# A trunk of four encoder layers on one core: settling an mLSTM head between the next one's reciprocal and additions, and the first and last chunks cut finer

## The chip, the cores and the metric

The kernel runs on 1 core of one Trainium2 chip. A core has TensorE (PE in the profile; PEld is its weight load), VectorE (DVE), ScalarE (ACT), GpSimd (POOL) and SyncE (SP), each of which works in order through its own queue, and 16 DMA engines. The metric is device time in microseconds (us) of one execution. Before the change it was 927.92 us, the median of 3 runs (927.56 to 928.36).

## What is computed

The input x has 256 tokens of 1024 features in float32. Two layers of three sublayers each follow; every sublayer is added to a scaled x and normalised. In layer 0 the mixer is a bidirectional mLSTM with 4 heads, in layer 1 a windowed attention:

```python
for l in range(DEPTH):                                       # DEPTH = 2
    x = layer_norm(ALPHA * x + 0.5 * swiglu(x, ffn_w_in[l, 0], ffn_w_out[l, 0]), ...)
    y = mlstm_mixer(...) if l % 2 == 0 else window_attention(...)
    x = layer_norm(ALPHA * x + y, ...)
    x = layer_norm(ALPHA * x + 0.5 * swiglu(x, ffn_w_in[l, 1], ffn_w_out[l, 1]), ...)
```

`swiglu` is `(silu(x @ Wg) * (x @ Wu)) @ w_out` with 2816 hidden features. In the mLSTM each head has 256 value features and two directions. With `num` and `den` of both directions, a head's output is

```python
h = num_f / max(|den_f|, e_f) + num_b / max(|den_b|, e_b)
h = (h - mean(h)) * rsqrt(var(h) + LN_EPS)                    # per token and head
out = sigmoid(o) * (h * norm_g);  y = out @ w_out
```

## The kernel before

**Number format and tiles.** Each float32 operand is cut into a high and a low part (`_hi`, `_lo`, type fp32r), and a product is three matmuls: high by high, high by low, low by high (`mm3`, L476). Tokens lie in two tiles of 128 (`xt[0]`, `xt[1]`); `xT_hi` and `xT_lo` hold the features on the partitions, made by transposes on TensorE against `ident` (`to_xT`, L505), after which ScalarE copies the high part and VectorE subtracts for the low one (`split_evac`, L495). PSUM tiles come from two rings of four banks, `pw` (`wbank`) and `py` (`ybank`).

**Weights.** `Weights` (L147) holds the list of all weight pieces, 128 x 1024 numbers (512 KB) each, in the order of use. SyncE loads them into a ring (`w_raw`, 4 buffers); ScalarE copies each into `w_hi` (`high`, L214) and VectorE makes `w_lo` (`low`, L238), after which the buffer is free and the next load is issued. For the very first piece, `high` and `low` work in two halves of 512 columns. Inside the feed-forward sublayers a planner (`Paced`, L52) counts costs of the instructions as they are written and decides where the next `w_hi` and `w_lo` go in the engines' order; elsewhere the order is written by hand, with `W.done(0, n)` or `spare()` as places where up to n pieces are split. All queues are worked off in order.

**Start.** ScalarE's queue issues the four loads of x (a half of 512 features of a token tile each), SyncE's queue the first weights. TensorE does 14 transposes of `ident` by itself (`warm(14)`), 4 of the first half of `xt[0]`, 8 more of `ident`, and then the first products of the first weight piece (`first_mm`, L629). The high part of that half of x is copied by VectorE, not by ScalarE, in this place alone.

**mLSTM heads (L1078 on).** The loop over the 4 heads h writes: a piece of the output gate's projection on TensorE, `scores(h)` (with `combine(h - 2)` inside), `mix(h - 1)`, `divide(h - 1)`, `settle(h - 2)`. In `mix` TensorE makes the four numerators (2 token tiles, 2 directions) and ScalarE the absolute denominators. In `divide` VectorE takes the maximum and the reciprocal, ScalarE scales the first direction into `hx`, and VectorE adds the second direction scaled (2 instructions of 128x256). `combine` makes mean and variance of a head on VectorE (`hst`, `hmv`, `hrs`), and POOL raises to the power -1/2. `settle` subtracts the mean and multiplies by that power, in place, on VectorE (2 instructions of 128x256). After the loop come `divide(3)`, `combine(3)`, `settle(2)`, the product with the output gate's sigmoid (`gate_out`, tiles `h<-h,sg`), `settle(3)` and, from L1112, the transposes of `hx[0]` and the output projection.

**End of a sublayer (`tail`, L559).** Each token tile's output is 128 x 1024 in two PSUM banks, `y[t][0]` and `y[t][1]` (512 columns each), summed over the last chunks in `todo` (6 of them at the very end, three matmuls each per half). For tile 1 the order is: the second half's first 3 chunks, the first half's 6, the second half's last 3. `Norm.half` (L533) adds a half to the scaled x and takes its statistics (`bn_stats`); `Norm.finish` (L538) combines them (`mv`), lets POOL make the power (`rs`), and applies the gain `ln_g` and the offset `ln_b` on VectorE. In the last sublayer both are done in two pieces of 512 columns, and SyncE stores each piece (`out_dram`).

Of the kernel before, what the change touches and what calls it, by code (L numbers as in the profile page):

```python
# [9 lines left out]
F32 = mybir.dt.float32  # L10
FR = mybir.dt.float32r
AF = mybir.ActivationFunctionType
OP = mybir.AluOpType
# [133 lines left out]
class Weights:  # L147
# [66 lines left out]
    def high(self):  # L214

        nc, i = self.nc, self.made
        p = self.plan[i]
        while self.half and (p["word"] not in self.raw or any(h[0] == p["needs"] for h in self.half)):
            self.low()
        while any(s_[0] == p["needs"] or p["word"] not in self.raw for s_ in self.sums):  # L220
            self.sum()
        if p["word"] not in self.raw:
            return False
        scale, raw = p["scale"], self.raw[p["word"]]
        hi = self.pool.tile([128, D], FR, name="w_hi", tag="w_hi", bufs=RING)
        if i == 0:
            for j in range(2):
                s_ = slice(j * 512, j * 512 + 512)
                nc.scalar.copy(hi[:, s_], raw[:, s_])
        elif scale is None:  # L230
            nc.scalar.copy(hi, raw)
        else:
            nc.scalar.activation(hi, raw, AF.Copy, scale=scale())
        self.half.append((i, hi))
        self.made += 1
        return True

    def low(self):  # L238

        nc = self.nc  # L240
        i, hi = self.half.pop(0)
        p = self.plan[i]
        k, scale, raw = p["k"], p["scale"], self.raw[p["word"]]
        lo = self.pool.tile([128, D], FR, name="w_lo", tag="w_lo", bufs=RING)
        if i == 0:
# [75 lines left out]
def trunk_kernel(ctx: ExitStack, tc: tile.TileContext, x, ffn_w_in, ffn_w_out, ln_g, ln_b, ml_w_in, ml_gate_b,  # L321
# [67 lines left out]
    for j, (kind, l, i, _) in enumerate(stages):  # L389
        if kind == "ffn":  # L390
            wi, wo = ffn_w_in[l, i], ffn_w_out[l, i]
            nth = iter(range(2 * UNITS))

            def down(n):
                for _ in range(n):
                    rows(wo, next(nth))

            for c0 in (0, F):
                for a in range(4):
                    wide(wi, a * 256, c0)  # L400
            for g in range(GROUPS):
                c0 = 512 + 768 * g
                for a in range(4):
                    beside(wi, a * 256, c0, F + c0)
                down(2)
                seven(wi, c0 + 256, F + c0 + 256, lambda i_: down(1) if g < GROUPS - 1 or i_ < 2 else None)
            down(6)
        elif kind == "mlstm":
            for c0 in (1024, 1536):
                for a in range(4):  # L410
                    wide(ml_w_in[0], a * 256, c0)
            for c0 in range(0, 1024, 256):
                for a in range(2):
                    narrow(ml_w_in[0], a * 512, c0)
            for c0 in (2048, 2560):
                for a in range(4):
                    wide(ml_w_in[0], a * 256, c0)
            for c in range(8):
                rows(ml_w_out[0], c, (lambda c=c: gcol[:, c:c + 1]))
        else:  # L420
            for c0 in (1024, 0):
                for a in range(4):
                    wide(at_w_in[0], a * 256, c0)
            for c0 in (512, 768):
# [103 lines left out]
    class Norm:  # L528
        def __init__(self, t, ca, eps, gb, last=False):
            self.t, self.ca, self.eps, self.gb, self.last = t, ca, eps, gb, last  # L530
            self.stats = state.tile([128, 2, 6], F32, name="stats", tag="stats", bufs=2)

        def half(self, h, y):  # L533
            z = xt[self.t][:, h * 512:(h + 1) * 512]
            nc.vector.scalar_tensor_tensor(z, z, self.ca, y, op0=OP.mult, op1=OP.add)
            nc.vector.bn_stats(self.stats[:, h], z)

        def finish(self, spare):  # L538
            mv = state.tile([128, 2], F32, name="mv", tag="mv", bufs=2)
            nc.vector.bn_aggr(mv, self.stats)  # L540
            rs = state.tile([128, 2], F32, name="rs", tag="rs", bufs=2)
            nc.vector.tensor_scalar(rs[:, 0:1], mv[:, 1:2], self.eps, None, op0=OP.add)
            nc.gpsimd.tensor_tensor(rs[:, 1:2], rs[:, 0:1], mhalf[:, 0:1], op=OP.pow)
            z = xt[self.t]
            cuts = [slice(0, 512), slice(512, D)] if self.last or self.t and LC[bound[0]] else [A]
            for s_ in cuts:
                nc.vector.scalar_tensor_tensor(z[:, s_], z[:, s_], mv[:, 0:1], self.gb[0][:, s_],
                                               op0=OP.subtract, op1=OP.mult)
            if len(cuts) == 1:
                W.done(0, spare)  # L550
            for s_ in cuts:
                nc.vector.scalar_tensor_tensor(z[:, s_], z[:, s_], rs[:, 1:2], self.gb[1][:, s_],
                                               op0=OP.mult, op1=OP.add)
                if self.last:
                    nc.sync.dma_start(out[0, tok(self.t), s_], z[:, s_])
            if len(cuts) > 1:
                W.done(0, spare)

    def tail(y, h, todo, first, norm, last, turn_at, between=None):  # L559

        def one(t, o, n):
            c, (i, w) = todo[t][n]
            mm3(y[t][o], h(c, t), pair(w, A, 0, slice(o * 512, o * 512 + 512)), first and n == 0, n == len(todo[t]) - 1)

        for o in range(2):
            for n in range(len(todo[0])):
# [9 lines left out]
        for j, (o, n) in enumerate(order):  # L576
            if j == full + turn_at:
                emit_x(0, last)
            one(1, o, n)
            if j >= half and (n < half) == (o == 0):  # L580
                W.done(todo[1][n][1][0] + 1, next(more))
            if n == full - 1:
                norm[1].half(o, y[1][o])
        norm[1].finish(1)
        W.done(most=TD[bound[0]])
        return lambda: emit_x(1, last)
# [5 lines left out]
    def ffn(l, i, n, pending, last):  # L592
        with ExitStack() as ph:
# [10 lines left out]
            start = pending is None  # L604
            if start:
                warm(14)
                to_xT(0, xt[0], ybank, (0,), nc.vector.tensor_copy)
                W.split(1)
                warm(8)
            hs, pieces = [], []  # L610

            def tr(hB, t, h):
# [15 lines left out]

            def first_mm(ps, a):  # L629

                def mm(t, i, j):
                    for k in (2 * a, 2 * a + 1):
                        nc.tensor.matmul(ps[t], xT[i][:, k, tok(t)], pieces[a][j][:, k % 2], start=i == j == k == 0,
                                         stop=False)

                if a == 1:
                    for t in range(2):
                        to_xT(t, xt[t], ybank, (1,))
                pieces.extend(W.take(1))
                mm(0, 0, 0)  # L640
                if a == 0:
                    to_xT(1, xt[1], ybank, (0,))
                    W.split(2)
                mm(0, 1, 0)
# [222 lines left out]
    def mlstm(l, n, pending, last):  # L867
        with ExitStack() as ph:
# [157 lines left out]
                        ys.append(y)  # L1026
                part[h] = den, ys

            def divide(h):
                den, ys = part.pop(h)  # L1030
                nc.vector.tensor_max(den, den, ecol[:, :, h:64:32])
                nc.vector.reciprocal(den, den)
                for t in range(2):
                    nc.scalar.activation(hx[t][:, h], ys[2 * t][:, 0:256], AF.Copy, scale=den[:, t, 0:1])
                for t in range(2):
                    hh = hx[t][:, h]
                    nc.vector.scalar_tensor_tensor(hh, ys[2 * t + 1][:, 0:256], den[:, t, 1:2], hh,
# [40 lines left out]
            for h in range(4):  # L1078
# [332 lines left out]
```

## Time and profile before

| | |
|---|---|
| median of 3 runs | 927.92 us (927.56 to 928.36) |
| the profiled execution | 928.32 us |
| its span, first to last instruction | 926.6 us |
| TensorE busy | 916.5 us (99%), 4506 matmuls |
| VectorE, ScalarE, POOL busy | 785.4, 544.4, 98.1 us |
| mean granted TensorE clock | 0.997 |
| from HBM | 185.68 MB |

A row of the timeline gives start and duration in us, engine, line, operation, tile written and tiles read, shapes, a count of merged instructions (x2), and in brackets the idle time of the engine before it with what ended it. Nearly all rows have line L138, that of a helper which records every operation, so groups are told apart by their tiles. Matmuls are pipelined: one row's duration overlaps the next, and the distance between starts is what one costs. A row of the stretches gives from and to, length, busy time and count of PE, PEld, DVE, ACT and POOL, granted clock, DMA share and GB/s. A row of one tile's view gives the shortest, median and longest duration in ns. The chain that ended last is followed back from the last instruction, at each step to what released it.

### The profile page before, as it was taken

The page shows a single profiled execution, that of the slowest core. Times are in us where ns is not written, and L with a number is a line of the kernel's source. Part 1 is how long each engine was busy: PE and PEld are TensorE (multiplying, and loading weights), DVE is VectorE, ACT ScalarE, POOL GpSimd, SP SyncE. Part 2 cuts the span into 40 slices and gives each one's busy share as a digit, 9 for nine tenths or more (in the row PEclk, how much of TensorE's full clock was granted, in tenths as well). Part 3 has the DMA queues.
Part 4 walks back from the last instruction along what each step waited for, and adds up shares of the span by engine and source line. Part 5 has one row for each costly group of instructions (what it writes and reads, how often), then busy time and mean ns, then how long its engine had stood idle before and what let it go on. Part 6 is the DMA issues. An engine that isn't in the chain of part 4 may idle for free.

```text
span 926.6 us, 12512 instructions
## 1 busy us (share of the span) xinstructions
PE 916.5 (99%) x4506; PEld 767.3 (83%) x4506; DVE 785.4 (85%) x948; ACT 544.4 (59%) x766; POOL 98.1 (11%) x144
## 2 busy tenths in 40 slices
PE   9999999999999999999999999999999999999996
PEld 7888888889988888888888888888888888888885
DVE  5899997886699799988887899988868878998875
ACT  5656756347664548565636566565569555757460
POOL 0010103011111010101010101010435300110100
PEclk9999999999999999999999999999999999999998
DMA  8979774646535949685558597737434385969421
GB/s 280 356 180 334 216 246 74 229 133 199 188 108 188 344 112 345 166 304 137 160 176 323 144 330 210 269 69 227 156 122 133 101 273 195 274 194 346 122 86 45
DMA packets 98461, 187.54 MB, mean 202 GB/s; under 512 B 6720, under 2 KB 37456, under 8 KB 98400
## 3 DMA queue, kind: packets, MB, share of 16 engines
q1 hardware_dynamic: 91072, 173.04, 54.7%
q0 software_dynamic: 6752, 12.66, 8.6%
q10 hardware_dynamic: 576, 1.05, 0.3%
q8 instruction: 35, 0.57, 0.2%
q14 instruction: 26, 0.21, 0.1%
HBM read 185.68 MB, written 1.05 MB: 202 GB/s over the span
## 4 chain that ended last, share of the span: by engine, by line
PE 87%; DVE 8%; ACT 2%; issue 2%; DMA 1%; POOL 0%; SPq 0%; DVEq 0%; ACTq 0%; POOLq 0%
PE pw L138 56%; PE py L138 30%; DVE w_lo L138 3%; DMA s_raw<-in_ffn_w_in_dram 1%; DVE x L138 1%; ACT w_hi L138 1%; DVE s_raw L138 1%; DVE h L138 1%; DVE stats L138 0%; DVE wt L138 0%; ACT h L138 0%; DVE a_lo L138 0%; DVE hst L138 0%; DVE e L138 0%; DVE S L138 0%
## 5 line engine op out<-in xcount | busy, mean ns | idle before, releaser
L138 DVE TENSOR_TENSOR w_lo<-w_raw,w_hi 128x1024 fp32r<-128x1024 f32 (+1 forms) x237 | 281.8, 1219 | 24.7 <-ACT w_hi L138 22.4
L138 ACT CAST w_hi<-w_raw 128x1024 fp32r<-128x1024 f32 (+1 forms) x237 | 241.7, 1050 | 81.7 <-PE py L138 27.1
L138 PE MATMUL pw<-w_hi,xT_hi 128*128 128x512 f32 x560 | 221.6, 397 | 0.0
L138 PE MATMUL pw<-w_hi,xT_lo 128*128 128x512 f32 x560 | 218.0, 390 | 0.0
L138 PE MATMUL pw<-w_lo,xT_hi 128*128 128x512 f32 x560 | 217.4, 390 | 0.0
L138 ACT CAST w_hi<-s_raw 128x1024 fp32r<-128x1024 f32 x144 | 148.1, 1052 | 80.6 <-DVE s_raw L138 44.0
L138 DVE TENSOR_TENSOR w_lo<-s_raw,w_hi 128x1024 fp32r<-128x1024 f32 x144 | 173.0, 1220 | 22.4 <-ACT w_hi L138 21.9
L138 PE MATMUL py<-w_hi,h_hi 128*128 128x512 f32 x352 | 138.0, 392 | 0.0
L138 PE MATMUL py<-w_lo,h_hi 128*128 128x512 f32 x352 | 137.1, 390 | 0.0
L138 PE MATMUL py<-w_hi,h_lo 128*128 128x512 f32 x352 | 137.1, 390 | 0.0
L138 PEld LDWEIGHTS pw<-w_hi,xT_lo 128*128 128x128 f32 x560 | 105.0, 188 | 22.4
L138 PEld LDWEIGHTS pw<-w_lo,xT_hi 128*128 128x128 f32 x560 | 105.3, 188 | 21.0 <-DVE w_lo L138 0.4
L138 PEld LDWEIGHTS pw<-w_hi,xT_hi 128*128 128x128 f32 x560 | 105.0, 188 | 20.2 <-ACT xT_hi L138 0.2
L138 DVE TENSOR_TENSOR s_raw<-s_raw 128x1024 f32<-128x1024 f32 x72 | 87.2, 1221 | 1.0
L267 POOL DMA_DIRECT2D s_raw<-in_ffn_w_in_dram x24 | 29.2, 1215 | 511.8 <-DVE w_lo L138 469.4
L138 PEld LDWEIGHTS py<-w_hi,h_lo 128*128 128x128 f32 x352 | 66.1, 188 | 13.9
L138 PEld LDWEIGHTS py<-w_lo,h_hi 128*128 128x128 f32 x352 | 66.1, 188 | 13.8 <-DVE w_lo L138 0.3
L138 PEld LDWEIGHTS py<-w_hi,h_hi 128*128 128x128 f32 x352 | 66.1, 188 | 13.5
L138 PE MATMUL pw<-w_hi,S_hi 128*128 128x512 f32 x192 | 74.7, 389 | 0.0
L138 PE MATMUL pw<-w_lo,S_hi 128*128 128x512 f32 x192 | 74.7, 389 | 0.0
L138 PE MATMUL pw<-w_hi,S_lo 128*128 128x512 f32 x192 | 74.7, 389 | 0.0
L138 DVE TENSOR_TENSOR h_lo<-pw,h_hi 128x512 fp32r<-128x512 f32 x44 | 30.2, 688 | 24.4 <-ACT h_hi L138 24.3
(206 smaller groups left out, 1087.6 us busy)
## 6 DMA issues: line engine op xcount, KB each, us to landing
w_raw<-in_ffn_w_out_dram SPq DMA_DIRECT2D x88, 512.0 KB, 5.2
s_raw<-in_ffn_w_in_dram SPq DMA_DIRECT2D x72, 512.0 KB, 6.2
w_raw<-in_ffn_w_in_dram SPq DMA_DIRECT2D x56, 512.0 KB, 5.2
w_raw<-in_ffn_w_in_dram SPq DMA_DIRECT2D x96, 256.0 KB, 4.2
s_raw<-in_ffn_w_in_dram POOLq DMA_DIRECT2D x24, 512.0 KB, 6.0
w_raw<-in_ml_w_in_dram SPq DMA_DIRECT2D x24, 512.0 KB, 4.6
w_raw<-in_at_w_in_dram SPq DMA_DIRECT2D x12, 512.0 KB, 4.7
w_raw<-in_ml_w_out_dram SPq DMA_DIRECT2D x8, 512.0 KB, 4.0
```

What stands on the lines that cost most here:

```text
L138: r = f(out, *args, **kw)
L267: nc.gpsimd.dma_start(t.rearrange("p (k f) -> p k f", k=self.words[w]["k"]), v, accum_op=OP.add)
```

## The change

Three places are changed.

1. **Start.** The first piece of the first sublayer comes by two transfers of 128x512 (256 KB) instead of one. The second piece too is split in two halves of 512 columns by `high` and `low`. Of the first half of `xt[0]`, two transposes go first into a `pw` bank and are taken from there (VectorE copies the high part); then all four are made in a `py` bank, of which the last two are taken (ScalarE copies) and which stays for later sums. Then come 6 transposes of `ident` instead of 8. The first products are ordered by k within the first piece.
2. **mLSTM.** `divide(h - 1)` writes `settle(h - 2)` between ScalarE's two scaled copies and VectorE's two additions, where it stood after the additions; for the last, `divide(3)` contains `settle(2)`, where it stood after `combine(3)`. ScalarE's, TensorE's and POOL's orders are as before there.
3. **End, last sublayer only.** For tile 1, the second half's first 3 chunks end their sum, which is added to the scaled x (`first`). The last 3 chunks are summed in two quarters of 256 columns in `pw` banks, each added and given statistics of its own (`quarter`), so that `finish` combines three groups. The offset goes in pieces of 512, 256 and 256, and ScalarE's queue stores the last one. The statistics tile is larger (128 instead of 48 bytes per partition).

```diff
-        if i == 0:
+        if i < 2:                      # in high and in low: two halves of 512 columns
...
-                    wide(wi, a * 256, c0)
+                    if j == c0 == a == 0:
+                        piece([two(wi, 0, 0)[:, k:k + 1] for k in range(2)], 2)
+                    else:
+                        wide(wi, a * 256, c0)
...
+        def first(self, h, y):
+            z = xt[self.t][:, h * 512:(h + 1) * 512]
+            nc.vector.scalar_tensor_tensor(z, z, self.ca, y, op0=OP.mult, op1=OP.add)
+
+        def quarter(self, h, q, y):
+            z = xt[self.t][:, h * 512 + q * 256:h * 512 + (q + 1) * 256]
+            nc.vector.tensor_add(z, z, y)
+            nc.vector.bn_stats(self.stats[:, h + q], z)
+            self.parts = 3
...
-            for s_ in cuts:
+            if self.parts == 3:
+                cuts = [slice(0, 512), slice(512, 768), slice(768, D)]
+            for n_, s_ in enumerate(cuts):
                 nc.vector.scalar_tensor_tensor(z[:, s_], z[:, s_], rs[:, 1:2], self.gb[1][:, s_],
                                                op0=OP.mult, op1=OP.add)
                 if self.last:
-                    nc.sync.dma_start(out[0, tok(self.t), s_], z[:, s_])
+                    (nc.scalar if n_ == 2 else nc.sync).dma_start(out[0, tok(self.t), s_], z[:, s_])
...
+            if last and j == full + half:
+                break
             one(1, o, n)
+            if last and j == half - 1:
+                norm[1].first(1, y[1][1])
...
+        if last:
+            for q in range(2):
+                yq = wbank((128, 256))
+                for n in range(half, full):
+                    c, (i, w) = todo[1][n]
+                    mm3(yq, h(c, 1), pair(w, A, 0, slice(512 + 256 * q, 768 + 256 * q)), n == half, n == full - 1)
+                norm[1].quarter(1, q, yq)
...
                 warm(14)
-                to_xT(0, xt[0], ybank, (0,), nc.vector.tensor_copy)
+                early = wbank((128, 2, 128))
+                for k in range(2):
+                    nc.tensor.transpose(early[:, k], xt[0][:, tok(k)], ident)
+                split_evac(pair(xT, A, slice(0, 2), tok(0)), early, high=nc.vector.tensor_copy)
+                late = ybank((128, 4, 128))
+                for k in range(4):
+                    nc.tensor.transpose(late[:, k], xt[0][:, tok(k)], ident)
+                turned[0, 0] = late
                 W.split(1)
-                warm(8)
+                split_evac(pair(xT, A, slice(2, 4), tok(0)), late[:, 2:4])
+                warm(6)
...
-                mm(0, 0, 0)
                 if a == 0:
+                    mm(0, 0, 0, (0,))
                     to_xT(1, xt[1], ybank, (0,))
                     W.split(2)
-                mm(0, 1, 0)
+                    mm(0, 1, 0, (0,))
+                    mm(0, 0, 0, (1,))
+                    mm(0, 1, 0, (1,))
...
-            def divide(h):
+            def divide(h, between=None):
                 den, ys = part.pop(h)
                 nc.vector.tensor_max(den, den, ecol[:, :, h:64:32])
                 nc.vector.reciprocal(den, den)
                 for t in range(2):
                     nc.scalar.activation(hx[t][:, h], ys[2 * t][:, 0:256], AF.Copy, scale=den[:, t, 0:1])
+                if between is not None:
+                    between()
...
-                    divide(h - 1)
-                if h > 1:
-                    settle(h - 2)
+                    divide(h - 1, (lambda: settle(h - 2)) if h > 1 else None)
...
-            divide(3)
+            divide(3, lambda: settle(2))
             combine(3)
-            settle(2)
             gate_out(0, 0)
```

The recorded order of each engine's instructions differs in these three places alone; between them it is the same, instruction by instruction.

More of the change, by code (lines that the diff above doesn't have):

```diff
@@ L244, in low @@
         lo = self.pool.tile([128, D], FR, name="w_lo", tag="w_lo", bufs=RING)
-        if i == 0:
+        if i < 2:
             for j in range(2):
@@ L530, in __init__ @@
             self.t, self.ca, self.eps, self.gb, self.last = t, ca, eps, gb, last
-            self.stats = state.tile([128, 2, 6], F32, name="stats", tag="stats", bufs=2)
+            self.stats = state.tile([128, 32], F32, name="stats", tag="stats", bufs=2)[:, 0:18].rearrange("p (h s) -> p h s", h=3)
+            self.parts = 2
         def half(self, h, y):
@@ L536, in half @@
             nc.vector.bn_stats(self.stats[:, h], z)
+        def first(self, h, y):
[6 more added lines that the diff above has]
+            self.parts = 3
         def finish(self, spare):
             mv = state.tile([128, 2], F32, name="mv", tag="mv", bufs=2)
-            nc.vector.bn_aggr(mv, self.stats)
+            nc.vector.bn_aggr(mv, self.stats[:, 0:self.parts])
             rs = state.tile([128, 2], F32, name="rs", tag="rs", bufs=2)
@@ L562, in one @@
             c, (i, w) = todo[t][n]
-            mm3(y[t][o], h(c, t), pair(w, A, 0, slice(o * 512, o * 512 + 512)), first and n == 0, n == len(todo[t]) - 1)
+            end = n == len(todo[t]) - 1 or last and t == o == 1 and n == len(todo[t]) // 2 - 1
+            mm3(y[t][o], h(c, t), pair(w, A, 0, slice(o * 512, o * 512 + 512)), first and n == 0, end)
         for o in range(2):
@@ L629, in first_mm, with mm @@
             def first_mm(ps, a):
-                def mm(t, i, j):
-                    for k in (2 * a, 2 * a + 1):
+                def mm(t, i, j, ks=(2 * a, 2 * a + 1)):
+                    for k in ks:
                         nc.tensor.matmul(ps[t], xT[i][:, k, tok(t)], pieces[a][j][:, k % 2], start=i == j == k == 0,
@@ L639, in first_mm @@
                 pieces.extend(W.take(1))
-                mm(0, 0, 0)
                 if a == 0:
+                    mm(0, 0, 0, (0,))
                     to_xT(1, xt[1], ybank, (0,))
                     W.split(2)
-                mm(0, 1, 0)
+                    mm(0, 1, 0, (0,))
+                    mm(0, 0, 0, (1,))
+                    mm(0, 1, 0, (1,))
+                else:
+                    mm(0, 0, 0)
+                    mm(0, 1, 0)
                 if a == 0:
```

## The prediction

> **What bounds the kernel now.** I read the page first (the chain that ended last), then the busy time by stretches, then the timeline of the three places that the change touches: the first 15 us, the heads of the mLSTM (246 to 278 us) and the last 20 us.
>
> ```profile
> PE 87%; DVE 8%; ACT 2%; issue 2%; DMA 1%; POOL 0%; SPq 0%; DVEq 0%; ACTq 0%; POOLq 0%
> ```
> ```profile
> 246.00:277.10 31.10, 30.39 (x168) 25.69 (x166) 27.80 (x64) 18.70 (x37) 5.00 (x4) 1.00 0.28 89
> 277.10:900.00 622.90, 622.42 (x3019) 518.38 (x3020) 538.71 (x632) 376.51 (x523) 68.37 (x100) 1.00 0.65 205
> ```
>
> TensorE bounds it: 87% of the chain. After 277.1 us it is busy 622.42 of 622.90 us, so whatever TensorE gains before that should reach the end, and what the other engines gain there is worth nothing. In the heads 0.71 us of it is idle (31.10 less 30.39), which overlapping records make look smaller than it is. The rest of what can be won is the ramp at the start and the work behind the last matmul.
>
> **Part 1, the start (first word and x by parts).** Estimate: 0.
>
> ```profile
> 5.34 1.14 ACT L138 CAST w_hi<-w_raw 128x512 fp32r<-128x512 f32 x2 [1.03 <-DMA w_raw<-in_ffn_w_in_dram]
> 5.34 1.81 PE L138 MATMUL py<-ident 128*128 128x128 f32 x8
> 5.59 0.69 DVE L138 CAST xT_hi<-py 128x512 fp32r<-128x512 f32 x1 [4.19 <-PE py L138]
> 6.91 0.71 PE L138 MATMUL pw<-w_hi,xT_hi 128*128 128x512 f32 x2
> 13.83 0.39 PE L138 MATMUL pw<-w_hi,xT_hi 128*128 128x512 f32 x1
> 14.20 0.50 PE L138 MATMUL pw<-w_lo,xT_hi 128*128 128x512 f32 x1
> ```
>
> Ahead of the first real matmul at 6.91, TensorE has 14 idle transposes, 4 of x and 8 idle ones: 26. The changed order has 14, 2, 4 and 6: 26 again (two of x are done twice, two idle ones fewer). Each takes 0.21 us here. The operands were there already: xT_hi at 5.59 + 0.69 = 6.28, both halves of w_hi at 6.48. Two transposes instead of four and 256 columns instead of 512 bring xT_hi's first part to about 5.6, and w_hi's first half comes with the first 256 KB transfer; both only lengthen a wait that TensorE does not make. Added: on ScalarE a copy of 256 columns (an estimate of 0.3, half of one of the two in 1.14) and a second split w_hi, on VectorE the same two splits, each split some 0.1 more than the whole. They lie in ScalarE's idle time before 5.34 and between the first copies; their cover is the four transposes of x1 and four matmuls. Without it they would cost up to 0.3. SyncE's queue gets one more issue (0.33 by the last issue's row, below), so words 2 to 4 are issued later by that, and in the order of the built program the fourth word's issue now waits for x's first landing. That lies before 5.34, as four transposes of x precede that row; the word is first used when the third word's twelve matmuls are done, 13.83 + 2.7 = 16.5, so I cost it at 0. The one stall left, 13.83 to 14.20 (0.37, where the last two rows of part 3's matmuls stand 0.23 apart) with the same again behind it, comes from the third word's w_lo, behind ScalarE's copies of x's second part, which are not moved. Ends: -0.25 (it goes) to +0.3.
>
> **Part 2, settling a head between the reciprocal and the additions.** Estimate: -0.87.
>
> ```profile
> 252.13 0.95 DVE L138 TENSOR_TENSOR a_lo<-wt,a_hi 128x768 fp32r<-128x768 f32 x1
> 253.19 0.18 DVE L138 RECIPROCAL den<-den 128x4 f32<-128x4 f32 x1
> 253.97 0.88 DVE L138 SCALAR_TENSOR_TENSOR h<-py,den,h 128x256 f32<-128x256 f32 x2 [0.60 <-ACT h L138]
> 254.76 0.73 DVE L138 TENSOR_SCALAR h<-h,hmv,hrs 128x256 f32<-128x256 f32 x2
> 260.69 0.75 DVE L138 BATCH_NORM_STATS2 hst<-h 128x6 f32<-128x256 f32 x2
> ```
> ```profile
> 252.31 1.34 POOL L1049 TENSOR_TENSOR hrs<-hrs,mhalf 128x2 f32<-128x2 f32 x1 [12.45 <-DVE hrs L138]
> 257.59 1.34 POOL L1049 TENSOR_TENSOR hrs<-hrs,mhalf 128x2 f32<-128x2 f32 x1 [3.94 <-DVE hrs L138]
> 262.00 1.60 POOL L1049 TENSOR_TENSOR hrs<-hrs,mhalf 128x2 f32<-128x2 f32 x1 [3.08 <-DVE hrs L138]
> 266.05 0.72 POOL L1049 TENSOR_TENSOR hrs<-hrs,mhalf 128x2 f32<-128x2 f32 x1 [2.44 <-DVE hrs L138]
> ```
> ```profile
> 261.77 1.28 DVE L138 SCALAR_TENSOR_TENSOR w_lo<-w_raw,gcol,w_hi 128x1024 fp32r<-128x1024 f32 x1
> 264.74 0.74 DVE L138 BATCH_NORM_STATS2 hst<-h 128x6 f32<-128x256 f32 x2
> 265.81 0.73 DVE L138 TENSOR_SCALAR h<-h,hmv,hrs 128x256 f32<-128x256 f32 x2
> 266.46 0.69 DVE L138 TENSOR_TENSOR h<-h,sg 128x512 f32<-128x512 f32 x1
> 268.70 0.69 DVE L138 TENSOR_TENSOR h<-h,sg 128x512 f32<-128x512 f32 x1
> ```
>
> VectorE waits 0.60 in each head, after the reciprocal, for ScalarE's scaled copies (253.37 to 253.97). The two settling instructions (0.65 from start to what follows, 265.81 to 266.46) move into that hole. But they need POOL's power, which ends at 252.31 + 1.34 = 253.65, not at 253.37: a new wait of 0.28 for POOL at the head of VectorE's queue, with the additions (0.79 likewise, 253.97 to 254.76), the next head's weighting and its statistics queued behind it. So:
> - head 2: settle at 253.69 (0.04 after POOL), additions at 254.34, and done at 255.13, where before both pairs were done at 254.76 + 0.65 = 255.41: -0.28.
> - head 3: POOL's result moves along, 258.93 - 0.28 = 258.65; settle 258.69, statistics at 260.13 instead of 260.69: -0.56.
> - last division: POOL 263.60 - 0.56 = 263.04; settle 263.08, statistics at 264.52 instead of 264.74: -0.22 only, as the settling was later before. It no longer stands ahead of the gating product, so that starts at 266.46 - 0.22 - 0.65 = 265.59: -0.87.
>
> ```profile
> 268.48 0.60 PE L138 MATMUL pw<-ident,h 128*128 128x128 f32 x4
> 269.54 0.63 PE L138 MATMUL pw<-ident,h 128*128 128x128 f32 x4 [0.46 <-DVE h L138]
> 276.45 0.40 PE L138 MATMUL py<-w_hi,xT_hi 128*128 128x512 f32 x1
> 277.08 0.50 PE L138 MATMUL py<-w_lo,xT_hi 128*128 128x512 f32 x1 [0.23 <-DVE w_lo L138]
> ```
> ```profile
> 269.51 0.60 ACT L138 ACTIVATE sg<-pw 128x512 f32<-128x512 f32 x1 [3.15 <-DVE h L138]
> ```
>
> What TensorE gets: the second four transposes wait for the product of 268.70. It would now end at 268.52, before the first four are through (about 268.92): 0.62 gone. Late next is the chain from that product over the sigmoid (269.51 to 268.64; it reuses the buffer that the product reads), ScalarE's copies of xT_hi and w_hi and four w_lo, one behind the other, to the last matmul group (277.08 to 276.21). TensorE alone would be there at 276.45 - 0.62 + 0.23 = 276.06, so this chain still ends last, and the gain is its 0.87. The DMA issues that follow each w_lo move with it. Ends: -1.02 (both waits of TensorE gone, 0.62 and 0.40) to -0.25 (first rival).
>
> Where POOL's power runs, the rows show what holds it: its end comes 0.56 after that of VectorE's a_lo (252.13 + 0.95 = 253.08 against 253.65), 0.55 after w_lo (263.05 against 263.60), and behind the settling instruction it takes 0.72. The Trainium skill, SBUF — State Buffer, section "SBUF: two separate sides", says that VectorE instructions with two SBUF inputs and POOL's instructions hold a shared port pair as an exclusive lock. The first two rows agree; by that rule head 3's power, which now meets the gating product and w_lo instead of a settling, could be held through both, and the sum would be -0.85 instead of -1.47. No row here shows a power between two such instructions.
>
> **Part 3, the end (quarters).** Estimate: -0.60.
>
> ```profile
> 918.47 0.39 PE L138 MATMUL py<-w_lo,h_hi 128*128 128x512 f32 x1
> 918.70 0.39 PE L138 MATMUL py<-w_hi,h_lo 128*128 128x512 f32 x1
> 919.12 0.69 DVE L138 SCALAR_TENSOR_TENSOR x<-x,py 128x512 f32<-128x512 f32 x1 [0.62 <-PE py L138]
> 920.58 0.21 DVE L138 BATCH_NORM_AGGREGATE mv<-stats 128x2 f32<-128x12 f32 x1
> 922.21 1.41 DVE L138 SCALAR_TENSOR_TENSOR x<-x,rs,ln_b 128x512 f32<-128x512 f32 x2
> ```
> ```profile
> 242.80 0.28 PE L138 MATMUL pw<-q_lo,k_hi 128*128 128x256 f32 x1
> 242.92 0.28 PE L138 MATMUL pw<-q_hi,k_lo 128*128 128x256 f32 x1
> ```
> ```profile
> L138 DVE SCALAR_TENSOR_TENSOR h<-py,den,h x8: 475/480/484, 247.5 to 264.3; 128x256 f32<-128x256 f32 x8
> L138 DVE BATCH_NORM_STATS2 hst<-h x8: 411/416/423, 251.1 to 265.1; 128x6 f32<-128x256 f32 x8
> ```
> ```profile
> 240.82 0.41 DVE L138 TENSOR_TENSOR wt<-pw,wt 128x256 f32<-128x256 f32 x1
> ```
> ```profile
> 923.65 0.33 SPq L555 DMA_DIRECT2D out_dram<-x  x1
> out_dram<-x SPq DMA_DIRECT2D x2, 256.0 KB, 2.0
> ```
>
> Nine 512-column matmuls (0.23 apart, so from 918.70 - 1.84 = 916.86) become eighteen of 256, 0.12 apart, though each loads other weights: the last starts at 916.86 + 17 x 0.12 = 918.90, and its sum is there 0.31 later (0.28 and 0.03) at 919.21, against 919.12. VectorE is not quite free by then: the other half's sum comes at 916.63 + 0.42 = 917.05 and takes its 1.46 (as from 919.12 to 920.58) until 918.5, then come the first quarter's addition (0.41) and statistics (0.42), until 919.3. The second quarter's take 0.41 + 0.42 with 0.03 between instructions: aggregation at 920.18 instead of 920.58, -0.40. The added 512-column `first` lies in VectorE's idle time before. The output row then goes in 512, 256, 256: the last two start 0.40 apart (0.88 less 0.48, row of 253.97) and end 1.54 after the start instead of 1.41: +0.13. The last transfer is 128 KB on ScalarE's empty queue. No row shows that size: its landing lies between 2.0 (nothing of it depends on size) and 1.0 (all of it does). I take 1.7, an estimate nearer to the first, since SyncE's two 256 KB issues, 0.66 apart by VectorE's pieces, land as far apart, so that at most a third of the 2.0 is transfer: -0.33. Together -0.60; ends -1.27 and -0.27.
>
> **Sum.** Against the profiled execution (928.32, span 926.6 and 1.7 around it): 0 - 0.87 - 0.60 = -1.47, 926.85. The median of the runs is 0.40 below that execution, so 926.45, or 926.4, as a median: 0.16% less. This kernel's measurement tells about 0.2% (1.86 us) from no change.
>
> **Rivals.**
> - *POOL's last power is held through the gating product and w_lo.* The product would run from 265.59 to 266.28 and w_lo (1.28) behind it to about 267.5, where the next settling is due. Held through the product alone, POOL's result comes at 266.28 + 0.55 = 266.83, in time; held through both it comes at 268.1, the settling slips by 0.6, the heads give -0.25, in all -0.85: 927.1. For: the two rows of 0.55 and 0.56. Against: the 0.72 row ended although the product of 266.46 had begun. 14%.
> - *More is won.* The start's stall goes and the last transfer lands in 1.3: -0.25 - 0.87 - 1.0 = -2.1, 925.8. For: every stall named has a VectorE or ScalarE cause; against: the fixed 26 transposes and the chain behind the sigmoid. 19%, all past -1.86.
> - *Slower: the settling's wait for POOL grows.* It now stands ahead of the additions in three divisions in a row. If POOL came x later in each, VectorE's chain loses 3x; at x = 0.5 the gain is spent, at 1.11 the kernel is 0.2% slower, at 1.28 (one more w_lo of 261.77) it is 3.84 - 1.47 = +2.37, 930.3. Against: while VectorE waits for POOL it runs nothing that could hold POOL. 4%.
> - *The change does not do what it says* (the quarters or the settling give nothing): 927.0 to 927.9, 5%.
>
> The forecast holds 58%. Range 925.5 to 927.5: from the upper ends taken together to the lock and a lost end. Faster 0.2, same 0.76 (forecast, lock, nothing given, rounded), slower 0.04.
>
> **What would show it.** Start: first 512-column matmul again at 6.9, stall near 14 as before. Heads: VectorE's wait after each reciprocal named POOL and about 0.3 instead of ScalarE and 0.60; the second four transposes follow the first without a wait; the last w_lo's matmul near 276.2, still waiting. End: aggregation 1.2 to 1.3 after the last matmul's start, the last landing about 1.7 after its issue. I am wrong if the first matmul moves, if POOL's last power takes over 1.5 us, or if stalls of TensorE between 277 and 900 us change.

## The result, and the profile after

The changed kernel takes 936.87 us (median of 5 runs, 936.68 to 937.73), the kernel before 928.36 us on the same chip (5 runs, 927.56 to 929.49). The ratio is 1.0095, with a 95% interval of 1.0081 to 1.0109: slower by 0.9%, where 0.16% less was forecast. (The ratios here and below are those on record; the quotient of the two medians differs from them by up to 0.0005.) The profiled execution took 937.73 us; its span is 936.0 us, 9.4 more than before.

```profile
core 0: 936.0 us, clock 0.997
```

The mean granted clock is the same 0.997 as before. The stretch from the last late matmul of the mLSTM to a matmul near the end (277.10 to 900.00 before) lies here between 279.20 and 909.08. The columns are from and to, length, busy time and count of PE, PEld, DVE, ACT, POOL, granted clock, DMA share, GB/s:

```profile
279.20:909.08 629.88, 629.49 (x3020) 519.46 (x3021) 539.45 (x633) 376.07 (x523) 68.28 (x100) 1.00 0.65 203
```

TensorE is as busy as before (all but 0.39 us of it), does the same 3,020 matmuls (3,019 recorded before) at a granted clock of 1.00, and takes 7 us longer. So no stall was added: the matmuls themselves come more slowly. The chain that ended last shows which ones. Its rows are start, length, engine, tile and number of instructions. In a matmul the stationary operand is the 128x128 tile that PEld loads, here a piece of `xT` or `h`, and the moving operand is the one of 512 columns, here always a weight `w`. First two neighbours of the kernel before (48 matmuls with `xT` as the stationary operand and 4 transposes; then 24 with `h`), then the same instructions of the changed kernel:

```profile
78.99 11.35 PE pw L138 x52
90.34 5.44 PE py L138 x24
```
```profile
80.05 11.38 PE pw L138 x52
91.44 5.59 PE py L138 x24
```

The 24 with `h` come 5.44 / 24 = 226.7 ns apart before and 5.59 / 24 = 232.9 ns after; the 52 with `xT` keep their time within 0.03 us. The kernel before has this many 128x512 matmuls with `h` and with `S` (another tile of the feed-forward stage) as stationary operand, in three groups of each kind (groups of instructions; the count stands behind the shape):

```profile
L138 PE MATMUL py<-w_hi,h_hi 128*128 128x512 f32 x352 | 138.0, 392 | 0.0
L138 PE MATMUL pw<-w_hi,S_hi 128*128 128x512 f32 x192 | 74.7, 389 | 0.0
```

3 x 352 + 3 x 192 = 1,632 at 6.2 ns are 10.1 us, an estimate from the one group of 24. Followed matmul by matmul, TensorE is 0.39 us ahead of the kernel before at 31 us, 2.99 behind at 267, 2.12 behind at 277 (the heads gain), 8.96 at 900 and 9.37 behind the last matmul. The 10.1, less the 0.39, the 0.87 of the heads and about 0.5 in the attention (whose `q` came to a better place, see the last experiment), is 8.3; the other 1.0 of the 9.37 is not accounted for.

Of these matmuls the three edited places touch only the last nine with `h`. But the statistics tile was enlarged, as the quarters need a third set of statistics: it has two buffers, and each grew from 64 to 128 bytes per partition (48 used bytes take 64). Every tile allocated behind it in SBUF moved by 128 bytes. In the built programs `h_hi` lies at byte 141,664 of a partition before and 141,792 after, that is at 96 and at 224 modulo 256 (the rest after division by 256); `xT_hi` (125,024) and the weights (`w_hi` from 34,912 on) did not move and lie at 96 modulo 256 in both.

### The profile page after: what moved, and what is told of

It is laid out like the page before. It is cut to its first block, busy times and chain, and to the rows that moved or that the text cites. A ratio compares the mean times of both kernels' runs of the same rounds, so it can differ in the third digit from the quotient of the medians.

```text
span 936.0 us, 12541 instructions
## 1 busy us (share of the span) xinstructions
PE 925.5 (99%) x4515; PEld 768.3 (82%) x4515; DVE 786.6 (84%) x954; ACT 544.2 (58%) x768; POOL 98.5 (11%) x144
## 4 chain that ended last, share of the span: by engine, by line
PE 84%; DVE 8%; DMA 3%; ACT 2%; issue 2%; POOL 1%; SPq 0%; DVEq 0%; ACTq 0%; POOLq 0%
PE pw L138 54%; PE py L138 30%; DVE w_lo L138 3%; DMA s_raw<-in_ffn_w_in_dram 2%; ACT w_hi L138 1%; DVE x L138 1%; DMA w_raw<-in_ffn_w_out_dram 1%; DVE h L138 1%; DVE stats L138 0%; POOL hrs L1093 0%; DMA x<-in_x_dram 0%; DMA w_raw<-in_ffn_w_in_dram 0%; DVE s_raw L138 0%; DVE wt L138 0%; DVE hst L138 0%
```

## The experiments

Theory A: the stationary operand at 224 modulo 256 is read more slowly. Rival B: the edited code slows TensorE's stream. Rival C: any shift costs. Rival D, a variant of A: what counts is the distance between the stationary and the moving operand. In the diffs below, `...` stands for what is left out.

**The change with `h` back at 96 modulo 256.**

```
-            self.stats = state.tile([128, 32], F32, ...
+            self.stats = state.tile([128, 48], F32, ...
```

> The changed kernel with the two statistics tiles 192 instead of 128 bytes wide per partition, and nothing else: every tile allocated behind them (the FFN's h and S among them) then lies 256 bytes behind its place in the kernel before, not 128. Theory A (the 128 bytes put the stationary operands of the FFN's matmuls at a place from which TensorE reads them more slowly; 224 modulo 256 slow, 96 modulo 256 fast): the 128x512 matmuls with h or S as stationary operand come 226.7 to 227.5 ns apart again, and the time is that of the change's other parts, 926.5 to 928.5 us. Rival B (the code of the change, its start, its heads or its quarters, slows TensorE's stream, wherever the tiles lie): 232 to 233 ns apart, and 936 to 938 us. Rival C (any shift from the old place costs, because h, S and the weights were placed well together): about 937 us.

Measured: 927.57 us against 928.66 for the kernel before, a ratio of 0.9991 (0.9982 to 0.9999). `h` and `S` lie 256 bytes further than in the kernel before, and so at 96 modulo 256. The chain's row of the same 24 matmuls:

```profile
90.06 5.44 PE py L138 x24
```

64 bytes more per buffer give back 9 us: B and C fall. What is left of the change is a small gain.

**The kernel before, with the statistics tile widened and nothing else.**

```
-            self.stats = state.tile([128, 2, 6], F32, ...)
+            self.stats = state.tile([128, 32], F32, ...)[:, 0:12].rearrange("p (h s) -> p h s", h=2)
```

> The kernel before, with nothing but its two statistics tiles widened from 64 to 128 bytes per partition, so that every tile behind them lies 128 bytes further, as in the changed kernel. Theory A: the FFN's matmuls with h or S come 232 to 233 ns apart, attention's with q 228 instead of 231.5 to 233.7, and the time is 936 to 939 us, nine to ten above the kernel before. Rival B (the code of the change): 227 ns apart and 928 us.

Measured: 938.14 us, ratio 1.0102 (1.0088 to 1.0116).

```profile
91.45 5.59 PE py L138 x24
```

The widened tile alone makes the whole loss, without a line of the change.

**Weights, `xT` and the stages' tiles moved together.**

```
-    mhalf = consts.tile([128, 2], F32, name="mhalf")
+    mhalf = consts.tile([128, 34], F32, name="mhalf")[:, 0:2]
```

> The kernel before with a constant tile of the start padded by 128 bytes per partition, so that the weights, x, xT, the statistics and all tiles of the stages lie 128 bytes further: stationary and moving operands keep their distance. Theory A in its plain form (the stationary operand's own place, 224 modulo 256, is the slow one): matmuls with xT slow down too, all of the FFN's come 232 to 233 ns apart, and the time is 944 to 952 us. Rival D (the distance between the stationary and the moving operand's place decides, half of 256 being bad): 227 ns as before, and 928 us. Rival B: 928 us too, so that this run separates A from D only if the second run is slow.

Measured: 929.09 us, ratio 1.0007 (0.9998 to 1.0016).

```profile
80.79 11.37 PE pw L138 x52
92.16 5.44 PE py L138 x24
```

`h`, `xT` and the weights all lie at 224 modulo 256 now, and nothing is slow. Theory A in its plain form falls; D stands.

**The weights moved against all the rest.** As the run before, and one of x's tiles widened by another 128 bytes, so that `xT`, `h` and `S` are back at 96 modulo 256 and only `w` lies at 224.

```
+    mhalf = consts.tile([128, 34], F32, name="mhalf")[:, 0:2]
...
-    xt = [state.tile([128, D], F32, ...) for t in range(2)]
+    xt = [state.tile([128, D + 32 * (1 - t)], F32, ...)[:, 0:D] for t in range(2)]
```

> The kernel before with the weights' tiles alone moved against the rest: all of them lie 128 bytes further (224 modulo 256), while x, xT, the statistics and every tile of the stages lie 256 bytes further, so at their old places modulo 256 (xT, h and S at 96). Theory D (what counts is the distance, modulo 256 bytes, between the stationary operand and the moving one, w): all 128x512 matmuls of h, S and xT with w become slow, 232 to 233 ns apart, some 2,800 of them at 5.5 ns or about 15 us, and the time is 940 to 950 us; attention's matmuls of q (at 224) with w come 227 to 229 ns apart instead of 231.5 to 233.7. Rival A (the stationary operand's own place) and rival E (the place of the stage's tiles against x, xT and the statistics): no change, 227 ns and 928 us.

Measured: 944.39 us, ratio 1.0168 (1.0155 to 1.0182).

```profile
80.31 11.61 PE pw L138 x52
91.92 5.60 PE py L138 x24
```

`h` has its old place modulo 256 and is slow; and `xT`, fast in the runs above, is slow too (11.61 against 11.35). A and E fall; it is the distance to the moving operand that decides.

One more rival is that other engines, which write the weights' tiles, get in TensorE's way. The last stretch speaks against it: there ScalarE is idle, VectorE works on x and its statistics alone, and no weight is loaded any more. From 913.0 us on, 25 distances between matmuls with `h` average 226.7 ns in the kernel before; from 923.0 us on, 24 average 232.6 ns in the kernel whose statistics tile alone was widened. So the loss is there while no other engine works on the weights or on `h`.

**Two more distances.**

```
+            self.stats = state.tile([128, 24], F32, ...)[:, 0:12]...     # h and S 64 bytes further
```

> The kernel before with its two statistics tiles widened from 64 to 96 bytes per partition: every tile behind them lies 64 bytes further, h and S at 160 modulo 256. No theory has a rule for this place yet; between the two known places it shows whether the slow reading sets in by steps of 64 bytes or only with the 128. If h and S are slow here as at 224, 936 to 939 us; if they are fast as at 96, 927.5 to 929; if it grows evenly with the distance, some 932 us with 229.5 ns from matmul to matmul. Rival B: 928 us.

Measured: 938.63 us, ratio 1.0110 (1.0094 to 1.0125).

```profile
90.83 5.60 PE py L138 x24
```

```
+            self.stats = state.tile([128, 40], F32, ...)[:, 0:12]...     # h and S 192 bytes further
```

> The kernel before with its two statistics tiles 160 bytes wide: every tile behind lies 192 bytes further, h and S at 32 modulo 256, with w at 96 as ever. Theory D in its plainest form (only a distance of 0 modulo 256 is fast): 232 to 233 ns from matmul to matmul and 936 to 939 us. Rival (the slow distances are those of 32 to 160 bytes ahead, so that a stationary operand at 32, behind w's place, is read fast): 227 ns and 928 us.

Measured: 933.65 us, in a single run.

```profile
91.90 5.49 PE py L138 x24
```

64 bytes cost as much as 128; 192 cost 5.49 / 24 = 228.8 ns, a third of the others' loss, as neither theory had it. Together, for stationary minus moving operand modulo 256: 0 is 226.7 ns (with the tiles 256 bytes further too, so a period of 512 is excluded), 64 is 233.3, 128 is 232.9, 192 is 228.8. Smaller distances than 64 were not tried.

**The heads alone.** The kernel before with the change's second part, all tiles in place.

```
-                    divide(h - 1)
+                    divide(h - 1, (lambda: settle(h - 2)) if h > 1 else None)
...
-            divide(3)
+            divide(3, lambda: settle(2))
```

> The kernel before with the change's second part alone: settle between the next head's reciprocal and its additions, all tiles at their old places. The theory of the prediction: TensorE's first matmul behind the heads comes 0.87 us earlier than before (in the changed kernel it gained 0.76 there), VectorE waits 0.25 to 0.35 us for POOL after each reciprocal, and the time is 0.75 to 0.9 us less: a ratio of 0.9990 to 0.9992. Rival (a gain won there is lost again by 930 us, in a wait for weights or at the end): the matmuls behind 300 us come as late as before, and the ratio is 1.000.

Measured: 927.62 us against 928.55, ratio 0.9989 (0.9981 to 0.9998). The timeline's rows (start, length, engine; in brackets the idle time before and what ended it):

```profile
253.82 0.73 DVE L138 TENSOR_SCALAR h<-h,hmv,hrs 128x256 f32<-128x256 f32 x2 [0.31 <-POOL hrs L1051]
268.62 1.03 PE L138 MATMUL pw<-ident,h 128*128 128x128 f32 x8
276.34 0.50 PE L138 MATMUL py<-w_lo,xT_hi 128*128 128x512 f32 x1 [0.23 <-DVE w_lo L138]
```

TensorE is 0.13 behind the kernel before at 262 us and 0.74 ahead at 277: a gain of 0.87, which is kept to the end (1.25 ahead at the last matmul; where the other 0.5 comes from was not looked into). The 0.87 is what the expectation's theory gave, and the ratio of 0.9989 is 0.0001 below its range; the rival falls, though the interval reaches 0.9998.

**The end, in two variants**, both with the statistics tile of the first experiment: the third store on SyncE's queue, and the last tile stored in halves.

```
-                    (nc.scalar if n_ == 2 else nc.sync).dma_start(out[0, tok(self.t), s_], z[:, s_])
+                    nc.sync.dma_start(out[0, tok(self.t), s_], z[:, s_])
```

> The changed kernel with the statistics tiles 192 bytes wide (the fast place) and the third store issued by SyncE instead of ScalarE. Theory: what the quarters won before the last store's landing was lost behind it, since ScalarE's store ends a wait of SyncE's that has seven others behind it (landing to end 1.30 us with the store on ScalarE, 0.88 in the kernel before): with all stores on SyncE the end comes 0.85 to 0.95 us after the last landing, the third store is issued at about the same time (SyncE has been free for 0.0 to 0.1 us), and from the last matmul to the end it is 7.2 to 7.35 us instead of 7.67. Rival (SyncE's three issues queue and the third lands 0.4 us later, which is why ScalarE was taken): 7.65 to 7.75 us.

```
-                cuts = [slice(0, 512), slice(512, 768), slice(768, D)]
+                cuts = [slice(0, 512), slice(512, D)]
```

> As the run before, but the last tile is finished and stored in two halves, as in the kernel before; only its matmuls, additions and statistics go by quarters. Theory (the aggregate comes 0.54 us earlier by the quarters, but the third piece costs VectorE and the queues 0.16 us and a half-sized store lands no sooner): from the last matmul to the end 7.05 to 7.2 us, against 7.62 in the kernel before. Rival (a smaller last store does shorten the end): 7.35 us or more.

Measured: 927.32 us (ratio 0.9985, 0.9975 to 0.9994) and 927.62 us (0.9990, 0.9981 to 0.9999), against 928.55; the two intervals overlap. From the end of the last matmul (its start and one distance between matmuls) to the end of the span the traces give 7.64 and 7.59 us, where 7.72 stood with the store on ScalarE and 7.66 in the kernel before (the 7.67 and 7.62 of the expectations end 0.05 earlier, with the start of the last instruction). Both expectations missed, and the numbers come out at or near those of the rivals (7.65 and 7.35 or more) without their mechanisms: the third store was not late (it lands 1.92 us after its issue), and the closing behind the last landing stayed at 1.27 and 1.34 us instead of falling to 0.9, so ScalarE's queue was not the reason. The trace of SyncE shows the true one. Its last instructions wait for its DMAs' eight semaphores in a fixed order, one every 0.06 us, and the DMAs take the semaphores in turn. In the kernel before the last store was on the one waited for last (the other waits were over when it landed); in these two it is on the second and on the first of them, so that six and seven waits come behind it. What moved it by one is the single transfer that the new start adds.

**Without the new start; and the start alone.** The first has the heads, the quarters and the two halves, statistics tile 192 bytes wide; the second is the kernel before with the change's first part.

> The change without its first part (the start is that of the kernel before), statistics tiles 192 bytes wide, last tile stored in two halves by SyncE. Theory of the closing waits: SyncE waits for its DMAs' eight semaphores in a fixed order, 0.06 us each, and the one transfer that the new start adds moves the last store from the semaphore waited for last to the one waited for first; without it the last store is on the last one again, and from the last store's landing to the end it is 0.88 to 0.95 us as in the kernel before, not 1.27 to 1.34. From the last matmul to the end then 7.12 to 7.25 us (7.66 before, 7.59 with the new start). With 0.74 from the heads the time is 1.15 to 1.3 us under the kernel before: a ratio of 0.9985 to 0.9989. Rival (the closing is longer because of the quarters or the pieces stored): 7.55 to 7.65 us.

> The kernel before with the change's first part alone, all tiles at their old places. Theory: the first 128x512 matmul comes between 6.3 and 7.3 us (before 6.9 to 7.9 over six profiled runs with the old start), the fortieth 16.9 to 17.9 (17.5 to 19.3), a gain of 0.0 to 0.6 us; and the closing takes 1.27 to 1.34 us behind the last landing in place of 0.88, as its one added transfer puts the last store on the semaphore that is waited for first. Together a ratio of 0.9996 to 1.0005. Rival to the closing: 0.88 us, from the last matmul to the end 7.66.

Measured: 927.36 us, ratio 0.9988 (0.9979 to 0.9997), and 928.36 us, ratio 0.9998 (0.9989 to 1.0007), against 928.87. Both are as the theories had them. SyncE's waits for the stores (what it waited for, us in total, times, longest), first in the kernel before, then with the old start and the quarters, then with the new start alone:

```profile
SPq L1407 <- DMA out_dram<-x: 1.2, 2, 0.6
```
```profile
SPq L1433 <- DMA out_dram<-x: 1.2, 2, 0.6
```
```profile
SPq L1423 <- DMA out_dram<-x: 1.6, 1, 1.6
```

Two waits, one for each store in its turn, and 0.91 us from the last landing to the end, with the old start; one wait of 1.6 for the first semaphore and 1.33 us to the end with the new one, although nothing at the end of that kernel was changed. From the last matmul: 7.16 and 8.07 us, against 7.66. The cause of the long closing is shown, and with the old start the quarters do gain 0.50 us at the end.

**Attention's tiles moved as well.** In the kernel before `q` of the attention lies at 224 modulo 256, its weights at 96. The kernel without the new start, with two small tiles widened:

```
-            qs_col = tile_([128, 4], F32, "qs_col")
+            qs_col = tile_([128, 40], F32, "qs_col")[:, 0:4]
...
-                es = tile_([128, 2, 2], F32, "es", bufs=3)
+                es = tile_([128, 40], F32, "es", bufs=3)[:, 0:4].rearrange("p (t a) -> p t a", t=2)
```

> As the run before, with two small tiles of the attention widened so that q and its neighbours, 224 modulo 256 in the kernel before, and the softmax's tiles all lie at 96 modulo 256 as w does. Theory D: the 78 recorded matmuls (of 96) of q with w come 227 to 229 ns apart instead of 231.5 to 234, which is worth 0.4 to 0.6 us, and the time is that much under the run before. Rival (attention is bound elsewhere, so the faster matmuls only wait): under 0.15 us.

Measured: 926.91 us, ratio 0.9984 (0.9975 to 0.9993), 0.45 under the kernel without the new start, though the two intervals overlap. A row of the chain with 48 of `q`'s 96 matmuls, from the first experiment (`q` at 224) and from this one (at 96):

```profile
727.63 12.06 PE py L138 x56
```
```profile
727.92 11.81 PE py L138 x56
```

0.25 us for 48, or 5.2 ns each: the rule that was found on `h` holds for a tile that the kernel before had in a slow place. Its ratio is the lowest here, but the intervals do not tell it from those of the other kernels under 1.000, the heads alone among them.

## Why the prediction was wrong

**The step that failed is the one that was not taken.** Part 3 counted the quarters' instructions and never priced the wider statistics tile that they need. "What bounds the kernel now" took the stretch with 622.42 busy of 622.90 us as one whose length is given, so that all that TensorE gains before it should reach the end. But a TensorE that is always busy can still be made slower: the stretch measured 629.88 us, and 1,632 x 6.2 ns = 10.1 us (estimated above) is what the moved tiles cost in the whole kernel. None of the rivals held it, as all of them looked for waits. Changed stalls between 277 and 900 us were named as a sign of error; the stalls hardly changed (0.48 us idle before, 0.39 after), and the loss came without them.

**Start: forecast 0, and nothing that can be measured came.** The first 128x512 matmul did move, from 6.91 to 6.50, but the change is not what moved it. Rows of the changed kernel (the transposes of x, then `ident`, then the first product):

```profile
5.49 0.60 PE L138 MATMUL py<-ident,x 128*128 128x128 f32 x4
5.93 0.82 PE L138 MATMUL py<-ident 128*128 128x128 f32 x6
6.50 0.48 PE L138 MATMUL pw<-w_hi,xT_hi 128*128 128x512 f32 x1
```

The six are 0.11 us apart, not 0.21 as in all of the prediction's rows. When the distance halves differs from run to run of either start. The old start, in the run with `h` and `S` 192 bytes further, and the new one, in the run with the third store on SyncE:

```profile
5.28 1.04 PE L138 MATMUL py<-ident 128*128 128x128 f32 x8
6.37 1.02 PE L138 MATMUL pw<-w_hi,xT_hi 128*128 128x512 f32 x2
```
```profile
6.41 1.14 PE L138 MATMUL py<-ident 128*128 128x128 f32 x6
7.30 0.48 PE L138 MATMUL pw<-w_hi,xT_hi 128*128 128x512 f32 x1
```

So the first product comes between 6.37 and 7.93 with the old start (nine traces) and between 6.32 and 7.30 with the new one (five), by the run. The assumption that "each takes 0.21 us here" was wrong as a fixed number. Nor is the forecast of 0 confirmed by a difference too small to measure: a wait stood against it that the prediction left out. In the changed kernel TensorE waits for x:

```profile
5.09 0.56 PE L138 MATMUL pw<-ident,x 128*128 128x128 f32 x2 [0.40 <-DMA x<-in_x_dram]
```

It begins the transposes of x at 5.03 to 5.23 us in all five traces with the new start, and at 4.49 to 4.60 in six of the nine with the old one (4.79, 5.25 and 5.45 in the others). Whether the divided first load is what delays x was not tested by itself. The one added transfer, costed at an issue, cost 0.42 us at the other end of the kernel.

**Heads: forecast -0.87, measured -0.87.** In the changed kernel:

```profile
256.60 0.74 DVE L138 TENSOR_SCALAR h<-h,hmv,hrs 128x256 f32<-128x256 f32 x2 [0.31 <-POOL hrs L1093]
268.47 0.69 DVE L138 TENSOR_TENSOR h<-h,sg 128x512 f32<-128x512 f32 x1
268.71 1.00 POOL L1093 TENSOR_TENSOR hrs<-hrs,mhalf 128x2 f32<-128x2 f32 x1 [2.78 <-DVE hrs L138]
271.48 1.03 PE L138 MATMUL pw<-ident,h 128*128 128x128 f32 x8
279.20 0.50 PE L138 MATMUL py<-w_lo,xT_hi 128*128 128x512 f32 x1 [0.24 <-DVE w_lo L138]
```

VectorE waits 0.31 for POOL (forecast 0.28) where it waited 0.60 for ScalarE; the eight transposes go without a pause; the last `w_lo` still ends last. TensorE goes from 2.99 behind to 2.12. The rival of the last power: it ends at 269.71, 0.55 after the gating product (268.47 + 0.69 = 269.16), and the `w_lo` at 269.07 did not hold it. That fits a power held through the product alone, as the forecast had it.

**End: forecast -0.60, measured +0.17.** Rows of the changed kernel, and its stores with size and median time from issue to landing:

```profile
928.18 0.29 PE L138 MATMUL pw<-w_hi,h_lo 128*128 128x256 f32 x1
928.51 0.42 DVE L138 TENSOR_TENSOR x<-x,pw 128x256 f32<-128x256 f32 x1
929.42 0.24 DVE L138 BATCH_NORM_AGGREGATE mv<-stats 128x2 f32<-128x18 f32 x1
931.09 1.53 DVE L138 SCALAR_TENSOR_TENSOR x<-x,rs,ln_b 128x512 f32<-128x512 f32 x3
```
```profile
out_dram<-x SPq DMA_DIRECT2D x3, 256.0 KB, 2.0
out_dram<-x SPq DMA_DIRECT2D x1, 128.0 KB, 2.1
out_dram<-x ACTq DMA_DIRECT2D x1, 128.0 KB, 2.0
```

Term by term, counted from the start of the second half's last chunks: the aggregation comes 0.42 earlier (forecast 0.40; it starts 1.24 after the last matmul's start); from it to the last issue it takes 3.23 instead of 3.07, +0.16 (forecast +0.13); the 128 KB land after 2.04, not 1.7, so +0.01 where -0.33 stood: half the bytes landed no sooner in these runs; and the closing takes 1.33 instead of 0.91, +0.42, which no step had.

**The sum without the wider tile** is 0 - 0.87 + 0.17 = -0.70; the first experiment, which is that kernel, measured a ratio of 0.9991, or -0.84 of 928.66 us, within an interval of -1.7 to -0.1. Taken from the 927.92 of the prediction that is 927.1, which would lie inside its range, but not for the prediction's reasons: the end lost 0.17 where it was to win 0.60. The mechanism of the change was read rightly at the heads, and half of it at the end (the earlier aggregation); the loss of 9 us came from where the tiles lie.

## What to carry to other kernels

A change in a tile's size is an edit of every address behind it: in a kernel with 128x512 fp32r matmuls like these, compare the places, modulo 256 bytes, of stationary and moving operands before and after, and pad a small tile so that they keep their distance. A stage in which TensorE is always busy can still slow down, so price the distance between matmuls and not only the gaps. Count the transfers too: one more at the start can move the last store to a semaphore whose wait has seven others behind it.

## What the runs showed of the hardware that was not expected

- The distance between 128x512 fp32r matmuls depends on where the stationary operand lies relative to the moving one: 226.7 ns at 0 modulo 256 bytes, 228.8 at 192, 232.9 at 128, 233.3 at 64. The Trainium skill, "TensorE: Matmul & The Clock Gate", section "Step-by-step: what each phase is for", says that TensorE has two independent read ports into SBUF, so that loading the next weights does not take bandwidth from the running matmul. These runs differ: with everything else alike, the places of the two operands make up to 6.6 ns in 227. Why (how the two reads meet in SBUF) no run here shows; it stays open.
- At the start 128-column transposes go from 0.21 to 0.11 us apart at a moment that differs between runs of like code: at 5.4 us in the changed kernel, at 7.05 in the run with the third store on SyncE. The same page, section "What's actually happening", says that TensorE's clock is halved until some 3.4 us of activity have passed, by a window that runs freely, so that the moment varies by 500 ns either way. The halved distance agrees; the spread is wider here. The profile's slices give a granted clock of 1.00 ahead of that moment too, but only because nothing is recorded there: the trace's record of the granted clock begins, with 1.00, at 5.39 and 7.06 us in these two, and at 4.5 to 9.5 us over all fourteen traces.
- A last store of 128 KB lands 1.92 to 2.04 us after its issue in these traces, one of 256 KB after 2.01 to 2.04.
